# Gate rows of a mixture step: one float32 product of a token against two accumulating float32r products

## The chip, the cores and the metric

One Trainium2 chip, one of its cores. The metric is the device time of one execution in microseconds. It was run three times before the change: 4808.69, 4848.3 and 4856.97 us, median 4848.3.

## The reference

A two-layer backbone runs over 128 context tokens and 512 latent tokens of width 1024. Each layer has a token mixer (four recurrent groups) and then PEER, a mixture of 16384 single-neuron experts, of which eight heads pick 16 each for a token. The part that matters here is PEER:

```python
def peer(h, lp):
    ...
    s1 = jnp.einsum("thd,kd->thk", q[:, :, 0], lp["peer_k1"].astype(f32))
    s2 = jnp.einsum("thd,kd->thk", q[:, :, 1], lp["peer_k2"].astype(f32))
    v1, i1 = lax.top_k(s1, PEER_TOPK)
    v2, i2 = lax.top_k(s2, PEER_TOPK)
    ...
    sc, pos = lax.top_k(cand, PEER_TOPK)
    eidx = jnp.take_along_axis(cidx, pos, axis=-1)
    gate = jax.nn.softmax(sc, axis=-1)
    ...
        act = jax.nn.gelu(jnp.einsum("td,thkd->thk", xb, ub).astype(f32), approximate=False)
        return jnp.einsum("thk,thkd->td", (gb * act).astype(vb.dtype), vb)
```

An expert's number is e1 * 128 + e2, with e1 and e2 from two tables of 128 keys.

## The kernel before

**How PEER is worked.** The 128 context tokens gather their experts' rows one by one (an indirect DMA by GpSimd, a dot product by VectorE). For the 512 latent tokens the kernel computes every expert's score instead: 128 blocks of 128 experts. `score` (L1621) loads a block's weights `u`, splits them into two float32r parts, `uh` (ScalarE, L1627) and `ul` (GpSimd, a subtraction, L1628), and runs 24 float32r products of 512 columns into one PSUM bank `S` (L1632 to L1634): eight k-blocks, high by high, high by low and low by high. ScalarE's gelu takes `S` to `ring` (L1636), which goes to DRAM. `dense` (L1733) later multiplies the scores by a table of gates and by the second weights.

**The gates.** `gates_dense` (L1589) makes that table for 128 tokens at a time: for each token a 128x128 matrix over (e2, e1), zero but for the token's 128 picks, into which each pick's gate is added. It is a product over the 128 picks: `A` is one where e2 of the pick equals the column, `B` is the gate where e1 equals the column. It goes in 32 steps of four tokens. In a step VectorE writes `A` (L1605) and `C` (L1607), each by one comparison of the index row `iota` with the four tokens' picks; ScalarE turns `C` into `B` in four instructions with the gate as the scale (L1610); TensorE runs one float32 product of 128 columns a token into the bank `G` (L1613); ScalarE copies the bank to `stg` (L1614), tokens innermost there: it reads PSUM in order, and writes with a stride of 128 elements. `A` and `B` have three buffers, `C` two, `G` four.

**Ticks.** The score blocks are spread over this work. `tick` (L1682) runs one block of scores, and then issues up to two gathers of rows (`fetch`, L1658, GpSimd, paced by the block's `ul`) and uses the rows that came (`use`, L1666: VectorE's dot products into `junk`, L1670, on at most two rows less than were issued). `gates_dense` calls a tick every second step, with two gathers; `route` (L1558), which picks the experts with top-16 instructions on VectorE, calls 20, 14, 9, 9 and 9 for its five tiles of tokens. What is left of the 128 blocks of a layer runs behind the last tile.

**What sets the order.** The code is written in this order, and a scheduler then places the instructions of each engine's queue with a time line of its own; the engines run their queues in order. So gate products stand between score products on TensorE, `B` between `uh`, the gelu and the copies on ScalarE, and `A`, `C`, the dot products and the next tiles' routing on VectorE. In this text a *dense tick* is one with two gate steps (eight tokens), a *thin tick* one with some three tokens, beside the routing of a tile or where that was.

**The split.** `split` (L308) copies a tensor to its float32r part (on whichever engine the scheduler takes) and subtracts that from the whole on VectorE.

Of the kernel before, what the change touches and what calls it, by code (L numbers as in the profile page):

```python
# [9 lines left out]
F32 = mybir.dt.float32  # L10
F32R = mybir.dt.float32r
# [3 lines left out]
AF = mybir.ActivationFunctionType  # L15
ALU = mybir.AluOpType
# [12 lines left out]
P = 128  # L29
# [22 lines left out]
def _const_blocks():  # L52
# [27 lines left out]
    c["sel"] = sel  # L80
    groups = {"A": ["ident", "bones", "dtm", "fm", "nfm", "sgn"], "G": ["mL0", "mL1"], "H": ["gs", "sel"]}
    groups["R"] = ["mA0", "mA1", "rs"]
# [173 lines left out]
class Kern:  # L256
# [776 lines left out]
    def rwkv_tail(self, Y, cx):  # L1033
        nc = self.nc
        for j in range(2):
            a, b = (cx.tile([P, 12 * 128], F32, name=f"A{d}")[:, :2 * T] for d in range(2))
            sg = b.rearrange("p (z t) -> p z t", z=2)
# [11 lines left out]
    def rw_prep(self, l, d, r, k, kk, th, la, rb, omk, PC, dp, ip, tp):  # L1049
# [7 lines left out]
        for j in range(2):  # L1057
# [32 lines left out]
            for i in od:  # L1090
                A = ip.tile([P, 2, 2, 3 * 64], F32, name="A")
                for a_ in range(2):
# [3 lines left out]
                    for b in range(2):  # L1096
                        nc.tensor.matmul(pv[:, b], bk[hr, i, 2 * b:2 * b + 2].rearrange("p s t -> p (s t)"),
                                         ar[hr, j, 2 * i + b].rearrange("p s t -> p (s t)"), start=True, stop=True)
                    nc.vector.tensor_tensor(A[:, :, a_, :P], pv, self.cst(f"mA{d}")[:, None, :].to_broadcast([P, 2, P]),
                                            op=ALU.mult)  # L1100
                for b in range(2):
                    rr = slice(b * 64, b * 64 + 64)
                    nc.sync.dma_start(ad[b, i, 2 * j:2 * j + 2].rearrange("h s t -> s h t"), A[rr, b, :, :64])
                ps = self.small()
                for b in range(2):
                    nc.tensor.transpose(ps[:, b * P:(b + 1) * P],
                                        bk[:, i, 2 * b:2 * b + 2].rearrange("p s t -> p (s t)"), self.ident)
                nc.scalar.copy(A[:, :, :, P:], ps[:, :2 * P].rearrange("p (b a n) -> p b a n", b=2, a=2))
                nc.sync.dma_start(self.sA[d][:, i, :, j], A.rearrange("p b a n -> p b (a n)"))
# [479 lines left out]
    def gates_dense(self, e1, e2, gt, t0, gd, tp):  # L1589
        nc = self.nc  # L1590
        sl = tp.tile([P, 3, P], F32, name="sl")
        ps = self.small()
        for j, a in enumerate((e1, e2, gt)):
            nc.tensor.transpose(ps[:, j * P:(j + 1) * P], a, self.ident)
        nc.scalar.copy(sl, ps[:, :3 * P].rearrange("p (j n) -> p j n", j=3))
        N = 4
        io = self.iota[:, None, :].to_broadcast([P, N, P])
        stg = self.stp.tile([P, P, P], F32, name="stg")
        for t in range(0, P, N):

            def bc(j):
                return sl[:, j, t:t + N][:, :, None].to_broadcast([P, N, P])

            A = tp.tile([P, N, P], F32, name="A", bufs=3)
            nc.vector.tensor_tensor(A, io, bc(1), op=ALU.is_equal)  # L1605
            C = tp.tile([P, N, P], BF16, name="C", bufs=2)
            nc.vector.tensor_tensor(C, io, bc(0), op=ALU.is_equal)  # L1607
            B = tp.tile([P, N, P], F32, name="B", bufs=3)
            for y in range(N):
                nc.scalar.activation(B[:, y], C[:, y], AF.Copy, scale=sl[:, 2, t + y:t + y + 1])  # L1610
            ps = self.psg.tile([P, N, P], F32, name="G")
            for z in range(N):
                nc.tensor.matmul(ps[:, z], A[:, z], B[:, z], start=True, stop=True)  # L1613
            nc.scalar.copy(stg[:, :, t:t + N].rearrange("p i t -> p t i"), ps)  # L1614
            if t // N % G_TICK == 0:
                self.tick(G_FETCH, 0)
        self.stg = stg
        if t0 < NS - P:
            self.gw += [(gd[i // 8][:, :, t0:t0 + P], stg[:, i:i + 8]) for i in range(P - 8, -1, -8)]
# [310 lines left out]
```

## Time and profile before

| | us |
|---|---|
| three runs | 4808.69, 4848.3, 4856.97 |
| the profiled execution | 4822.85 |
| its span, first to last instruction | 4821.1 |
| layer 1's stretch with the gates | 930 to 1640 |
| layer 2's stretch with the gates | 3300 to 4020 |

The profile has one execution's instructions on each engine, with start, length, form, what they read and wrote, and what ended the idle time before them. PE is TensorE's products, PEld its loads of weights, DVE is VectorE, ACT ScalarE, POOL GpSimd, SP SyncE. A name ending in q is the sequencer's own instruction. A group's idle time is that of the engine just before its instructions. The ends of products are modelled, so their starts are the better measure. A float32 product appears as two records, a float32r product as one.

### The profile page before, as it was taken

Reading aid. Unit: us, or ns where it says so; the run is one execution under the profiler, and the core shown is the slowest. Engines: PE = TensorE matmul, PEld = TensorE weight load, DVE = VectorE, ACT = ScalarE, POOL = GpSimd, SP = SyncE. Lnnn points to the kernel's source line nnn. Section 1 sums busy time; section 2 is a strip of 40 time slices with the busy share of each in tenths; the row PEclk is TensorE's granted clock in tenths of the full one; section 3 lists DMA queues with packets and bytes.
Section 4 is the critical chain, followed back from the end, with each engine's and each line's share of the span. In section 5 each row is a group of like instructions: output and inputs, shape, how many; then the busy total and the mean of one; then the engine's idle time right before and its main releaser. Section 6 shows DMA issues by size and latency. Waiting matters only on the chain. (4 is left out here: it accounts for less than half of the span.)

```text
span 4821.1 us, 64797 instructions
## 1 busy us (share of the span) xinstructions
PE 4481.7 (93%) x23050; PEld 3702.0 (77%) x23050; DVE 3525.9 (73%) x6251; ACT 1912.1 (40%) x3357; POOL 2384.7 (49%) x1287
## 2 busy tenths in 40 slices
PE   7998979999999998998989899999999999999987
PEld 5786768788888876776767776887878887877775
DVE  7785478978854699996777766699795665555677
ACT  3433233446665522222233233434656664222222
POOL 2221133465666566776643212434755665665664
PEclk8996579999999999999999985999999999999998
DMA  5666141368788788888834673323878886787785
GB/s 194 189 183 205 57 143 64 123 206 268 257 274 275 254 278 297 296 282 262 296 129 120 188 222 96 119 83 117 266 252 261 267 279 229 243 257 259 257 290 175
DMA packets 504279, 1025.97 MB, mean 213 GB/s; under 512 B 80017, under 2 KB 247185, under 8 KB 502801
## 3 DMA queue, kind: packets, MB, share of 16 engines
q1 hardware_dynamic: 280112, 592.70, 38.3%
q0 software_dynamic: 75328, 275.02, 17.4%
q10 hardware_dynamic: 148514, 154.10, 9.4%
q8 instruction: 181, 2.97, 0.3%
q14 instruction: 144, 1.18, 0.1%
HBM read 841.41 MB, written 180.24 MB: 212 GB/s over the span
## 5 line engine op out<-in xcount | busy, mean ns | idle before, releaser
L1628 POOL TENSOR_TENSOR ul<-u,uh 128x1024 fp32r<-128x1024 f32 x256 | 658.6, 2573 | 661.2 <-ACT uh L1627 556.5
L1753 PE MATMUL O<-q,vh 128*128 128x512 f32 x2048 | 819.9, 401 | 102.9 <-DVE q L1775 102.4
L1754 PE MATMUL O<-qh,vl 128*128 128x512 f32 x2048 | 807.6, 395 | 23.5 <-POOL vl L1762 23.5
L1634 PE MATMUL S<-hh,ul 128*128 128x512 f32 x2048 | 813.5, 397 | 12.1 <-POOL ul L1628 12.0
L1632 PE MATMUL S<-hh,uh 128*128 128x512 f32 x2048 | 813.0, 397 | 9.3 <-ACT ring L1636 9.3
L1752 PE MATMUL O<-qh,vh 128*128 128x512 f32 x2048 | 804.3, 394 | 7.7 <-ACT qh L1774 5.3
L1762 POOL TENSOR_TENSOR vl<-v,vh 128x1024 fp32r<-128x1024 f32 x256 | 669.9, 2618 | 280.1 <-ACT vh L1761 272.2
L1633 PE MATMUL S<-hl,uh 128*128 128x512 f32 x2048 | 804.2, 393 | 0.0
L1753 PEld LDWEIGHTS O<-q,vh 128*128 128x128 f32 x2048 | 390.3, 191 | 228.5 <-DVE q L1775 148.8
L1772 DVE TENSOR_TENSOR h<-h,gt 128x384 f32<-128x384 f32 x250 | 272.1, 1089 | 372.5 <-issue 267.8
L310 POOL TENSOR_TENSOR wl<-w,wh 128x1024 fp32r<-128x1024 f32 (+1 forms) x106 | 239.1, 2261 | 551.5 <-ACT wh L309 459.2
L1774 ACT CAST qh<-h 128x512 fp32r<-128x512 f32 x250 | 154.7, 620 | 883.7 <-DVE h L1773 583.3
L1627 ACT CAST uh<-u 128x1024 fp32r<-128x1024 f32 x256 | 268.0, 1047 | 579.9 <-PE S L1633 292.6
L1670 DVE SCALAR_TENSOR_TENSOR junk<-row,hpr 128x1024 bf16<-128x1024 f32 x256 | 361.9, 1414 | 184.7 <-DMA row<-in_u_dram,ix 175.3
L1754 PEld LDWEIGHTS O<-qh,vl 128*128 128x128 f32 x2048 | 390.6, 191 | 108.4 <-POOL vl L1762 30.0
L1662 POOL DMA_INDIRECT row<-in_v_dram,ix x256 | 320.2, 1251 | 288.7 <-DVE hpr L1678 251.7
L1752 PEld LDWEIGHTS O<-qh,vh 128*128 128x128 f32 x2048 | 390.1, 191 | 92.6 <-ACT qh L1774 6.5
L1634 PEld LDWEIGHTS S<-hh,ul 128*128 128x128 f32 x2048 | 387.6, 189 | 94.1 <-POOL ul L1628 14.9
L1632 PEld LDWEIGHTS S<-hh,uh 128*128 128x128 f32 x2048 | 387.9, 189 | 85.1 <-ACT ring L1636 10.9
L1633 PEld LDWEIGHTS S<-hl,uh 128*128 128x128 f32 x2048 | 387.4, 189 | 77.3
L1678 DVE SCALAR_TENSOR_TENSOR hpr<-row,act,hpr 128x1024 f32<-128x1024 f32 x254 | 395.5, 1557 | 1.1
L296 PE MATMUL mm<-hh,wh 128*128 128x320 f32 x1184 | 383.4, 325 | 12.7 <-ACT hh L443 9.0
(449 smaller groups left out, 8639.1 us busy)
## 6 DMA issues: line engine op xcount, KB each, us to landing
u<-in_ub_dram SPq DMA_DIRECT2D x256, 512.0 KB
v<-in_v_dram SPq DMA_DIRECT2D x256, 512.0 KB
sd<-ring ACTq DMA_DIRECT2D x250, 256.0 KB
h<-sd SPq DMA_DIRECT2D x250, 256.0 KB
gd<-stg ACTq DMA_DIRECT2D x96, 512.0 KB
gt<-gd SPq DMA_DIRECT2D x256, 192.0 KB
modw<-in_modw_dram SPq DMA_DIRECT2D x88, 512.0 KB
w<-in_win_dram SPq DMA_DIRECT2D x58, 512.0 KB
```

The costliest lines, as they stand in the source:

```text
L296: nc.tensor.matmul(t[:m, :HT], a, b[:, sl], start=k == 0, stop=k == n - 1)
L1628: pp = nc.gpsimd.tensor_sub(ul, u, uh.bitcast(F32))
L1632: nc.tensor.matmul(ps, uh[:, k], xh, start=k == 0, stop=False)
L1633: nc.tensor.matmul(ps, uh[:, k], xl, start=False, stop=False)
L1634: nc.tensor.matmul(ps, ul[:, k], xh, start=False, stop=k == KC - 1)
L1662: nc.gpsimd.indirect_dma_start(out=r, out_offset=None, in_=self.I[tab], in_offset=bass.IndirectOffsetOnAxis(ap=ix[:, s:s + 1], axis=0))
L1670: nc.vector.scalar_tensor_tensor(junk, r, 1.0, hp, op0=ALU.mult, op1=ALU.mult, accum_out=act[:, s:s + 1])
L1678: nc.vector.scalar_tensor_tensor(out, r, act[:, s:s + 1], out, op0=ALU.mult, op1=ALU.add)
L1752: nc.tensor.matmul(acc[c], vh[:, sl], qh, start=z == 0, stop=False)
L1753: nc.tensor.matmul(acc[c], vh[:, sl], q, start=False, stop=False)
L1754: return nc.tensor.matmul(acc[c], vl[:, sl], qh, start=False, stop=z == NB - 1)
L1762: pace = nc.gpsimd.tensor_sub(vl, v, vh.bitcast(F32))
```

## The change

`A`, `B` and the gate become float32r. The gate row of a tile is split once into a high and a low part, `gh`. `B` gets two halves a token: the first is written by ScalarE as before, with the high part as the scale; the second by VectorE, in one instruction a token, from the index row: it compares `iota` with the pick and multiplies by the low part. TensorE then runs two float32r products of 128 columns a token on the same `A`, the second adding to the first. The copy to `stg` reads PSUM with tokens innermost (a stride of 128 elements) and writes four tokens side by side.

```diff
+        gh = tp.tile([P, 2, P], F32R, name="gh")
+        self.split(gh[:, 0], gh[:, 1], sl[:, 2])
+        gf = gh.bitcast(F32)
         stg = self.stp.tile([P, P, P], F32, name="stg")
         for t in range(0, P, N):
...
-            A = tp.tile([P, N, P], F32, name="A", bufs=3)
+            A = tp.tile([P, N, P], F32R, name="A", bufs=3)
             nc.vector.tensor_tensor(A, io, bc(1), op=ALU.is_equal)
             C = tp.tile([P, N, P], BF16, name="C", bufs=2)
             nc.vector.tensor_tensor(C, io, bc(0), op=ALU.is_equal)
-            B = tp.tile([P, N, P], F32, name="B", bufs=3)
+            B = tp.tile([P, N, 2, P], F32R, name="B", bufs=3)
             for y in range(N):
-                nc.scalar.activation(B[:, y], C[:, y], AF.Copy, scale=sl[:, 2, t + y:t + y + 1])
+                z = t + y
+                nc.scalar.activation(B[:, y, 0], C[:, y], AF.Copy, scale=gf[:, 0, z:z + 1])
+                nc.vector.tensor_scalar(B[:, y, 1], self.iota, sl[:, 0, z:z + 1], gf[:, 1, z:z + 1],
+                                        op0=ALU.is_equal, op1=ALU.mult)
             ps = self.psg.tile([P, N, P], F32, name="G")
             for z in range(N):
-                nc.tensor.matmul(ps[:, z], A[:, z], B[:, z], start=True, stop=True)
-            nc.scalar.copy(stg[:, :, t:t + N].rearrange("p i t -> p t i"), ps)
+                nc.tensor.matmul(ps[:, z], A[:, z], B[:, z, 0], start=True, stop=False)
+                nc.tensor.matmul(ps[:, z], A[:, z], B[:, z, 1], start=False, stop=True)
+            nc.scalar.copy(stg[:, :, t:t + N], ps.rearrange("p t i -> p i t"))
```

VectorE's queue in the dense ticks of a tile of the first layer, before (`junk` is the dot product of a gathered row):

```order
L1670 SCALAR_TENSOR_TENSOR junk,act<-row,hpr 128x1024
L1605 TENSOR_TENSOR A<-iota,sl 128x512 x2
L1670 SCALAR_TENSOR_TENSOR junk,act<-row,hpr 128x1024
L1607 TENSOR_TENSOR C<-iota,sl 128x512 x2
L1670 SCALAR_TENSOR_TENSOR junk,act<-row,hpr 128x1024
L1605 TENSOR_TENSOR A<-iota,sl 128x512 x2
L1670 SCALAR_TENSOR_TENSOR junk,act<-row,hpr 128x1024
```

The same place of VectorE's queue in the changed kernel, in whose line numbers A is L1608, C L1610, the second half of B L1615 and the dot product L1677:

```order
L1677 SCALAR_TENSOR_TENSOR junk,act<-row,hpr 128x1024
L1608 TENSOR_TENSOR A<-iota,sl 128x512
L1615 TENSOR_SCALAR B<-iota,sl,gh 128x128 x4
L1608 TENSOR_TENSOR A<-iota,sl 128x512
L1615 TENSOR_SCALAR B<-iota,sl,gh 128x128 x4
L1677 SCALAR_TENSOR_TENSOR junk,act<-row,hpr 128x1024
L1610 TENSOR_TENSOR C<-iota,sl 128x512 x2
```

Four new instructions stand behind each A; between them the dot products, A and C keep their places.

TensorE's queue at a thin tick of the first layer's last tile, before (S is the score, G the gates):

```order
L1632 MATMUL S<-hh,uh 128x512
L1633 MATMUL S<-hl,uh 128x512
L1613 MATMUL G<-B,A 128x128 x3
L1634 MATMUL S<-hh,ul 128x512
L1632 MATMUL S<-hh,uh 128x512
```

And in the changed kernel, where the scores are L1639 to L1641 and the two products of a token L1619 and L1620:

```order
L1640 MATMUL S<-hl,uh 128x512
L1619 MATMUL G<-B,A 128x128
L1620 MATMUL G<-B,A 128x128
L1619 MATMUL G<-B,A 128x128
L1620 MATMUL G<-B,A 128x128
L1619 MATMUL G<-B,A 128x128
L1641 MATMUL S<-hh,ul 128x512
```

Three products of three tokens became five of two and a half; they stay between the same score products, and a dense tick holds 16 where it held eight.

## Rows read from the trace of the kernel before

**Rows 1.** The page's head: span, then busy us, share and instructions of each engine.

```profile
span 4821.1 us, 64797 instructions
...
PE 4481.7 (93%) x23050; PEld 3702.0 (77%) x23050; DVE 3525.9 (73%) x6251; ACT 1912.1 (40%) x3357; POOL 2384.7 (49%) x1287
```

**Rows 2.** Windows of the two stretches: length, PE, PEld, DVE, ACT, POOL busy, clock, DMA, GB/s.

```profile
930.00:1640.00 710.00, 704.63 (x3591) 599.01 (x3592) 512.18 (x763) 437.05 (x865) 440.87 (x235) 1.00 0.77 250
3300.00:4020.00 720.00, 711.04 (x3630) 604.84 (x3629) 508.88 (x749) 439.97 (x870) 438.79 (x236) 1.00 0.77 250
```

**Rows 3.** Timeline of TensorE's products over a dense tick: start us, length us.

```profile
1423.21 1.95 PE L1613 MATMUL G<-B,A 128*128 128x128 f32 x16
...
1425.23 0.39 PE L1633 MATMUL S<-hl,uh 128*128 128x512 f32 x1
1425.46 0.39 PE L1634 MATMUL S<-hh,ul 128*128 128x512 f32 x1
...
1430.46 1.95 PE L1613 MATMUL G<-B,A 128*128 128x128 f32 x16
```

**Rows 4.** Groups by line, 930 to 1640 us: count, busy us, mean ns, idle before.

```profile
L1613 PE MATMUL G<-B,A 128*128 128x128 f32 x1016 | 130.6, 275 | 0.0
L1613 PEld LDWEIGHTS G<-B,A 128*128 128x128 f32 x1016 | 129.9, 191 | 8.7
L1607 DVE TENSOR_TENSOR C<-iota,sl 128x512 bf16<-128x512 f32 x128 | 129.9, 1035 | 38.5 <-ACT B L1610 38.5
```

**Rows 5.** Timeline of VectorE over the same tick.

```profile
1425.79 2.02 DVE L1670 SCALAR_TENSOR_TENSOR junk<-row,hpr 128x1024 bf16<-128x1024 f32 x1 [1.62 <-DMA row<-in_u_dram,ix]
...
1427.74 1.28 DVE L1605 TENSOR_TENSOR A<-iota,sl 128x512 f32<-128x512 f32 x2
1428.95 1.25 DVE L1670 SCALAR_TENSOR_TENSOR junk<-row,hpr 128x1024 bf16<-128x1024 f32 x1
...
1430.13 1.28 DVE L1607 TENSOR_TENSOR C<-iota,sl 128x512 bf16<-128x512 f32 x2
```

**Rows 6.** Timeline of GpSimd over the same tick.

```profile
1424.35 2.39 POOL L1628 TENSOR_TENSOR ul<-u,uh 128x1024 fp32r<-128x1024 f32 x1 [1.71 <-ACT uh L1627]
...
1431.59 2.41 POOL L1628 TENSOR_TENSOR ul<-u,uh 128x1024 fp32r<-128x1024 f32 x1 [1.71 <-ACT uh L1627]
```

**Rows 7.** Timeline of TensorE: float32r products of 320 columns, four between left out.

```profile
99.95 0.31 PE L296 MATMUL mm<-hl,wh 128*128 128x320 f32 x1
...
100.83 0.31 PE L296 MATMUL mm<-hl,wh 128*128 128x320 f32 x1
```

**Rows 8.** Timeline of TensorE's loads of weights: products of 65 columns.

```profile
2926.18 0.74 PEld L867 LDWEIGHTS sm<-vx,w 128*128 128x128 f32 x6 [1.48 <-DVE w L855]
```

**Rows 9.** Timeline of TensorE: a pair of records after an idle time.

```profile
462.51 0.43 PE L869 MATMUL sm<-mst,qs 64*128 64x65 f32 x2
```

**Rows 10.** Single lines of VectorE: count, ns min/median/max, first and last start, form.

```profile
L587 DVE TENSOR_SCALAR raw<-sp,cstA x2: 596/596/597, 102.3 to 2521.8; 64x640 f32<-64x640 f32 x2
L485 DVE TENSOR_SCALAR gr<-ge x2: 484/486/487, 78.8 to 2506.7; 64x640 f32<-64x640 f32 x2
L1574 DVE TENSOR_SCALAR ab<-pos x20: 210/220/2432, 866.9 to 3562.4; 128x128 uint32<-128x128 uint32 x20
L1523 DVE MAX8 s<-mr x80: 365/428/431, 846.1 to 3556.0; 128x8 f32<-128x256 f32 x80
```

**Rows 11.** Single lines of ScalarE: a read of a PSUM bank in order; the copy to stg.

```profile
L1636 ACT ACTIVATE ring<-S x256: 582/592/625, 818.3 to 4026.5; 128x512 f32<-128x512 f32 x128
L1614 ACT COPY stg<-G x256: 1058/1083/1172, 944.4 to 4010.5; 128x512 f32<-128x512 f32 x128
```

**Rows 12.** Windows: a run of thin ticks, columns as in rows 2.

```profile
1300.00:1360.00 60.00, 59.27 (x292) 49.70 (x292) 20.42 (x26) 33.61 (x60) 23.40 (x10) 1.00 0.87 269
```

**Rows 13.** Waits, 930 to 1640 us: us in total, times, longest us.

```profile
DVE A L1605 <- PE G L1613: 33.0, 11, 8.5
```

## The prediction

> **What bounds the kernel now.** I read the head of the page first: TensorE is busy 93% of the span, every other engine less [rows 1]. The change touches only the stretch in which the gates of the 512 latent tokens are built, once in each layer; I cut that out of the table of windows. There TensorE is busy 704.6 of 710 us and 711.0 of 720 us, at a granted clock of 1.00 (its 2.4 GHz level), while VectorE is busy 512 and 509 us [rows 2]. So a microsecond that TensorE loses in these 1430 us is a microsecond of the kernel, and one that it saves counts only if nothing else is late next.
>
> Then I read the stretch as a period, in the timeline. In the dense part one tick goes with two gate steps: 24 score products and eight tokens. The gate products are one row of 16 records from 1423.21 us, and the next such row begins at 1430.46: a period of 7.25 us [rows 3]. The records of one row stand (1.95 - 0.275) / 15 = 0.112 us apart; 1024 tokens give 2048 records [rows 3, 4]: each float32 product runs as two records, 0.223 us a token. A score product comes 0.227 us after the last [rows 3].
>
> In the same period VectorE works: two A (1.21 us from the first start to what follows), a dot product (1.18), two C (1.2) and a second dot product (1.2), 4.8 us in all [rows 5]. GpSimd's subtraction for `ul` takes 2.39 us [rows 6]. These two exclude each other: the dot product that starts at 1425.79 takes 2.02 us instead of 1.25, and ends 1.07 us after the subtraction's end at 1426.74 [rows 5, 6]; C averages 1035 ns in this stretch though the pair takes 1.28 [rows 4, 5]. Before that dot product VectorE idled 1.62 us for its gathered row [rows 5], and that idle time lies beside the subtraction. So 4.8 + 2.4 = 7.2 us of the 7.25 are already taken on VectorE. TensorE is the bound, but VectorE with GpSimd is a second one at almost the same height. This is the main point of the forecast.
>
> **The change part by part.** *The products.* 1024 float32 products go, 2048 float32r products of 128 columns come: as many records as now. The trace has no float32r product under 320 columns. Bounds: going by columns alone, 320 take 0.147 us start to start (six in 0.88 us) and 512 take 0.227, 0.42 ns a column, so 128 would take 0.067 us [rows 3, 7]. But each record also loads 128 columns of weights. The loads of the 65-column products on 128x128 weights stand (0.74 - 0.19) / 5 = 0.110 us apart, as far as the gates' records of 128 columns [rows 3, 8]: there the load, not the columns, sets the pace. Two such products in a row after an idle time even stand 0.43 - 0.27 = 0.16 us apart [rows 4, 9]. I take 0.111 us, the row nearest in kind (back-to-back, 128x128 weights, few columns): 2048 x (0.112 - 0.111) is nothing. Ends: -0.045 x 2048 = -92 us and +0.048 x 2048 = +98 us.
>
> The Trainium skill, TensorE: Matmul & The Clock Gate, section "LDWEIGHTS (loading the stationary operand)", prices a load by its columns alone, 107 ns for 128; the 0.110 us of rows 8 agree. The same page's section "Back-to-back issue gap" gives about 81 ns a product for a sustained stream at 128 columns; by that TensorE would save some 63 us (an estimate from that page). No row here shows 128-column loads closer than 0.11 us, so the trace sides with the first rule.
>
> *The second half of B on VectorE.* 1024 one-input TENSOR_SCALAR of 128 columns with two pointer scalars are added, eight a dense tick. A 640-column one with two pointers takes 596 ns; without pointers 640 columns take 486 and 128 columns 220 [rows 10]. The slope is 266 / 512 = 0.52 ns a column, so 596 - 266 = 330 ns, less the 0.08 us by which neighbours on VectorE overlap (a pair of A takes 1.28, not 2 x 0.68): 0.25 us each, 2.0 us a tick. Bounds: 0.14 us (the 220 ns without pointers) and 0.33 us. Does it run beside GpSimd's subtraction? A TENSOR_SCALAR of the same size stretches from 220 to 2432 ns in this stretch, MAX8 never goes past 431 [rows 10]. So it waits like A and C do.
>
> The Trainium skill, SBUF — State Buffer, section "Who interferes with whom", says that a VectorE instruction with one SBUF input is free of GpSimd outside the two-port modes, and that tensor_scalar can enter those. If these ran in the free mode, up to 2.0 us a tick would lie under the subtraction and the change would cost nothing; if not, it costs the sum below. The 2432 ns of rows 10 speak for the second.
>
> *The order.* In the changed kernel VectorE's queue reads dot product, A, four TENSOR_SCALAR, A, four more, dot product, two C; nothing else changes place. Behind a late TENSOR_SCALAR wait A, C and the dot products; behind a late C wait ScalarE's B and, queued behind those, the cast `uh`, then GpSimd's `ul`, then the score products. A late VectorE therefore stops TensorE as a whole, not just the gates.
>
> *ScalarE.* B stays four instructions a step. The copy to `stg` now writes four tokens side by side and reads PSUM with the stride: between 592 ns (an unstrided read of 128x512 from PSUM) and 1083 + 491 ns if the strided read costs what the strided write did [rows 11]. Two a tick: -1.0 to +1.0 us on an engine busy 437 of 710 us [rows 2]. I cost it at nothing: VectorE's period of 9.2 us (below) covers it, and without that cover it would cost up to 1.0 us less what ScalarE idles now. *The split of the gate row:* two short instructions a tile, eight tiles, at most 5 us, beside score products: nothing. A as float32r: same elements, nothing.
>
> **The sum.** Dense tick: 4.8 + 2.0 + 2.4 = 9.2 us of VectorE with GpSimd against 7.2 now: +2.0 us. The new TensorE order holds 92 ticks' worth of eight tokens (736 of the 1024) over both layers: +184 us. Taken off: in the thin ticks (three tokens) VectorE idles (20.4 busy of 60 us) and runs ahead until A has no free buffer (33 us of waits for the gate products) [rows 12, 13]. It enters six of the eight dense parts some two steps ahead, 7 us: -42 us. Added: in two tiles of each layer the thin ticks lie beside routing, with VectorE full; 44 ticks x 3 x 0.25 = 33 us, of which I take half: +16. Sum: +158 us. The profiled execution took 4822.9 us, which gives 4981; it lies 25 us under the median of the three runs (4848.3), on which scale it would be 5006. I say 4995.
>
> **The rivals.**
> *Hidden (no change).* The TENSOR_SCALAR slip under GpSimd's subtraction or into VectorE's idle 1.62 us, and TensorE still sets 7.25. For it: MAX8, also with one input, is never stretched, and no TENSOR_SCALAR of this very form is in the trace. Against: the stretched ones of rows 10, and that the idle time lies beside the subtraction. Time: 4823 to 4848.
> *Faster.* The float32r records run at 0.067 us, as the columns say. TensorE's dense tick falls to 24 x 0.227 + 16 x 0.067 = 5.45 + 1.07 = 6.5 us. For it: the column slope, which nothing in the trace breaks between 320 and 512. Against: rows 8. It decides only once VectorE with GpSimd falls below 7.2, that is if the additions are free and the dot products move under the subtraction too; then the whole -92 us counts: 4731 to 4756. (The Trainium skill's 81 ns, TensorE: Matmul & The Clock Gate, section "Back-to-back issue gap", belongs to this rival.) If only the additions are free, 7.2 stands, and the gain is that of the 288 tokens outside the dense ticks, 288 x 2 x 0.045 = 26 us, within what can be told from no change.
> *Dearer products.* The second product of a token waits for the first, 0.16 us a record [rows 9]. Against it: the score products accumulate too, and follow each other without a gap [rows 3]. The dense tick of TensorE is then 5.45 + 16 x 0.16 = 8.0, still under 9.2, so only the thin ticks pay: 288 x 2 x 0.048 = +28 us on top of the forecast, 5023; where a record costs a whole float32 product, 0.223, the dense tick is 9.0 and the thin tokens cost 288 x 0.223 = +64: 5059.
>
> **How the numbers follow.** Forecast 0.65; hidden 0.16; dearer products 0.11; faster 0.08. A measurement of this kernel tells about 1% from no change (4800 to 4897). Faster by more: the last case, 0.08. Within it: the hidden case and 0.02 of the forecast, where an addition costs least, 0.18. Slower by more: 0.63 and 0.11, 0.74. The likeliest case alone spans 4905 to 5120: 0.14 us an addition makes 92 x 1.1 - 42 + 9 = +68, and 0.33 us without any lead makes 92 x 2.6 + 44 = +283, each between the two scales. The whole range is 4815 (hidden, with a part of the 26 us of cheaper products) to 5145 (the +283 on the median's scale and a little for dearer products); the faster case lies outside it.
>
> **What would show it.** Right: the gate products' records still 0.11 us apart; the new TENSOR_SCALAR near 330 ns at the median with some over 2 us; dense ticks of about 9 us with VectorE full and TensorE idle before gate products, waiting for B; the two stretches each some 80 us longer and all else as it was. Wrong: records at 0.06 us; a dense tick that stays at 7.25 us; TENSOR_SCALAR that never stretch; time lost outside the two stretches; or ScalarE's copy as what the gate products wait for.

## The result and the profile after

The changed kernel takes 4981.35 us (median of four executions, 4944.74 to 4987.46) against 4832.22 (four executions of the kernel before beside them): a ratio of 1.029, 95% interval 1.025 to 1.034. It is slower by 2.9%. The forecast was 4995 us.

The head of the changed kernel's page, as [rows 1]:

```profile
span 4981.5 us, 65843 instructions
...
PE 4555.3 (91%) x23050; PEld 3754.3 (75%) x23050; DVE 3927.4 (79%) x7283; ACT 1811.7 (36%) x3363; POOL 2374.6 (48%) x1287
```

The span grows by 160.4 us. TensorE has as many products as before, 23050; VectorE has 1032 instructions and 402 us more; ScalarE is busy 100 us less. The two stretches with the gates, as [rows 2] (length, PE, PEld, DVE, ACT, POOL busy, clock, DMA, GB/s):

```profile
930.00:1720.00 790.00, 743.09 (x3621) 626.85 (x3620) 720.30 (x1261) 390.57 (x871) 432.77 (x236) 0.96 0.70 226
3390.00:4180.00 790.00, 739.98 (x3595) 623.64 (x3594) 713.71 (x1250) 389.68 (x870) 429.87 (x235) 0.95 0.70 227
```

The stretches became 790 us long, from 710 and 720. TensorE now idles some 50 us in each, at a lower granted clock, and VectorE, idle 198 of 710 us before, idles 70 of 790. The gates' products span 698.6 us before and 774.7 now in the first layer, 697.7 and 775.1 in the second (first to last start): 153.5 of the 160.4 us are in there.

TensorE's timeline at the gate products of a dense tick (start us, length us), as [rows 3]:

```profile
1494.66 0.40 PE L1641 MATMUL S<-hh,ul 128*128 128x512 f32 x1
1494.90 0.22 PE L1619 MATMUL G<-B,A 128*128 128x128 f32 x1
1494.96 0.27 PE L1620 MATMUL G<-B,A 128*128 128x128 f32 x1
1495.07 0.28 PE L1619 MATMUL G<-B,A 128*128 128x128 f32 x1
1495.18 0.28 PE L1620 MATMUL G<-B,A 128*128 128x128 f32 x1
...
1496.52 0.28 PE L1620 MATMUL G<-B,A 128*128 128x128 f32 x1
1496.63 0.44 PE L1639 MATMUL S<-hh,uh 128*128 128x512 f32 x1
```

From the second record to the last it is 1.56 us for 14 steps, 0.111 us each: what the float32 records took in [rows 3]. VectorE's new instructions (count, ns min/median/max, first and last start):

```profile
L1615 DVE TENSOR_SCALAR B<-iota,sl,gh x1024: 328/335/3000, 936.2 to 4167.9; 128x128 fp32r<-128x128 f32 x171
```

VectorE over one dense tick, as [rows 5], from one A to the A that stands at the same place of the next tick:

```profile
1494.65 0.68 DVE L1608 TENSOR_TENSOR A<-iota,sl 128x512 fp32r<-128x512 f32 x1
1495.26 1.10 DVE L1615 TENSOR_SCALAR B<-iota,sl,gh 128x128 fp32r<-128x128 f32 x4
1496.28 0.68 DVE L1608 TENSOR_TENSOR A<-iota,sl 128x512 fp32r<-128x512 f32 x1
1496.88 3.18 DVE L1615 TENSOR_SCALAR B<-iota,sl,gh 128x128 fp32r<-128x128 f32 x4
1499.99 1.21 DVE L1677 SCALAR_TENSOR_TENSOR junk<-row,hpr 128x1024 bf16<-128x1024 f32 x1
...
1501.13 1.28 DVE L1610 TENSOR_TENSOR C<-iota,sl 128x512 bf16<-128x512 f32 x2
1502.34 1.21 DVE L1677 SCALAR_TENSOR_TENSOR junk<-row,hpr 128x1024 bf16<-128x1024 f32 x1
...
1503.48 0.68 DVE L1608 TENSOR_TENSOR A<-iota,sl 128x512 fp32r<-128x512 f32 x1
```

The tick is 1503.48 - 1494.65 = 8.83 us, without an idle moment on VectorE. Over all 88 dense ticks of the trace VectorE idles less than 0.1 us a tick on the mean; in e1 below, which has the same order without the additions, it idles 1.46 of 7.25 us. Four additions take 1.02 us start to start where nothing is beside them (1495.26 to 1496.28), and 3.11 us at 1496.88. GpSimd says why, as [rows 6]:

```profile
1488.15 2.49 POOL L1635 TENSOR_TENSOR ul<-u,uh 128x1024 fp32r<-128x1024 f32 x1 [3.17 <-ACT uh L1634]
...
1496.96 2.50 POOL L1635 TENSOR_TENSOR ul<-u,uh 128x1024 fp32r<-128x1024 f32 x1 [3.17 <-ACT uh L1634]
```

The subtraction begins 0.08 us behind the first of these four. That first one still takes its usual 335 ns; the second, begun at 1497.14, takes 2412 ns, and ends 0.09 us behind the subtraction. And ScalarE's timeline shows what a late C holds up (in brackets: the idle time before, and what ended it):

```profile
1493.02 0.40 ACT L1614 ACTIVATE B<-C,gh 128x128 fp32r<-128x128 bf16 x1 [3.99 <-DVE C L1610]
...
1494.67 1.27 ACT L1614 ACTIVATE B<-C,gh 128x128 fp32r<-128x128 bf16 x4
1495.85 1.03 ACT L1634 CAST uh<-u 128x1024 fp32r<-128x1024 f32 x1
```

C, then B, then the cast `uh`, then `ul`: the ring is closed, since `ul` stops VectorE, which makes the next C late. In the list of waits (us in total, times, longest us) of the first stretch:

```profile
POOL ul L1635 <- ACT uh L1634: 271.1, 89, 8.8
ACT B L1614 <- DVE C L1610: 170.6, 44, 9.3
```

### The profile page after: what moved, and what is told of

Its sections match the earlier page's. It is cut to its first block, busy times and chain, and to the rows that moved or that the text cites. A ratio compares the mean times of both kernels' runs of the same rounds, so it can differ in the third digit from the quotient of the medians.

```text
span 4981.5 us, 65843 instructions
## 1 busy us (share of the span) xinstructions
PE 4555.3 (91%) x23050; PEld 3754.3 (75%) x23050; DVE 3927.4 (79%) x7283; ACT 1811.7 (36%) x3363; POOL 2374.6 (48%) x1287
## 5 line engine op out<-in xcount | busy, mean ns | idle before, releaser
L1641 PE MATMUL S<-hh,ul 128*128 128x512 f32 x2048 | 829.7, 405 | 20.7 <-POOL ul L1635 20.6
L1639 PE MATMUL S<-hh,uh 128*128 128x512 f32 x2048 | 831.0, 406 | 15.6 <-ACT ring L1643 15.6
L1640 PE MATMUL S<-hl,uh 128*128 128x512 f32 x2048 | 822.5, 402 | 0.0
L1615 DVE TENSOR_SCALAR B<-iota,sl,gh 128x128 fp32r<-128x128 f32 x1024 | 507.9, 559 | 0.0
L1641 PEld LDWEIGHTS S<-hh,ul 128*128 128x128 f32 x2048 | 398.9, 195 | 106.6 <-POOL ul L1635 23.3
L1639 PEld LDWEIGHTS S<-hh,uh 128*128 128x128 f32 x2048 | 400.9, 196 | 96.3 <-ACT ring L1643 18.8
L1640 PEld LDWEIGHTS S<-hl,uh 128*128 128x128 f32 x2048 | 399.9, 195 | 82.6
L1614 ACT ACTIVATE B<-C,gh 128x128 fp32r<-128x128 bf16 x1024 | 327.1, 393 | 360.1 <-DVE C L1610 353.3
```

Of the source, the lines that this page charges most:

```text
L1614: nc.scalar.activation(B[:, y, 0], C[:, y], AF.Copy, scale=gf[:, 0, z:z + 1])
L1615: nc.vector.tensor_scalar(B[:, y, 1], self.iota, sl[:, 0, z:z + 1], gf[:, 1, z:z + 1], op0=ALU.is_equal, op1=ALU.mult)
L1639: nc.tensor.matmul(ps, uh[:, k], xh, start=k == 0, stop=False)
L1640: nc.tensor.matmul(ps, uh[:, k], xl, start=False, stop=False)
L1641: nc.tensor.matmul(ps, ul[:, k], xh, start=False, stop=k == KC - 1)
```

## The experiments

Times are medians; the ratio is to executions of the kernel before on the same chip (medians of 4820 to 4836 us). The span of the gates is that of their products in the first layer, first to last start. The dense tick is counted in the trace, from the first of 24 score products to the next such first, where eight tokens' gate products start in between; its median stands here.

| kernel | us | ratio, 95% interval | span of the gates, us | dense tick, us |
|---|---|---|---|---|
| before | 4832 | 1 | 698.6 | 7.25 |
| changed | 4981 | 1.029, 1.025 to 1.034 | 774.7 | 8.83 |
| e1_no_low | 4842 | 1.006, 1.004 to 1.007 | 704.6 | 7.25 |
| e2_added | 5009 | 1.040, 1.036 to 1.043 | 787.9 | (other order) |
| e3_copy | 4828 | 1.000, 0.996 to 1.003 | 708.2 | 7.25 |
| e4_one | 4792 | 0.994, 0.992 to 0.997 | 684.1 | 6.46 |
| e5_psum | 4968 | 1.028, 1.025 to 1.032 | 773.8 | 8.44 |
| e6_act | 4844 | 1.000, 0.997 to 1.003 | 710.7 | 7.25 |
| e7_no_ul | 4862 | 1.007, 1.004 to 1.010 | 716.3 | 7.25 |
| e8_before_no_ul | 4861 | 1.005, 1.002 to 1.009 | 705.4 | 7.25 |
| e9_one_c16 | 4790 | 0.990, 0.987 to 0.993 | 676.2 | 6.72 |
| e10_half | 4885 | 1.009, 1.006 to 1.013 | 727.5 | 7.91 |
| e11_double | 5301 | 1.096, 1.093 to 1.099 | 940.5 | 11.25 |
| e12_one_no_ul | 4734 | 0.978, 0.973 to 0.982 | 643.8 | 6.35 |

**e1_no_low: without the additions.**

```diff
-                nc.vector.tensor_scalar(B[:, y, 1], self.iota, sl[:, 0, z:z + 1], gf[:, 1, z:z + 1],
-                                        op0=ALU.is_equal, op1=ALU.mult)
...
-                nc.tensor.matmul(ps[:, z], A[:, z], B[:, z, 1], start=False, stop=True)
+                nc.tensor.matmul(ps[:, z], A[:, z], B[:, z, 0], start=False, stop=True)
```

> The changed kernel without VectorE's 1024 new instructions: both products of a token read the first half of B (the low part of the gate is left out, the high part counts twice). TensorE, ScalarE and the copy work as in the changed kernel. Theory (the new instructions, together with GpSimd's subtraction, fill VectorE): the dense tick returns from 8.8 to about 7.25 us, each stretch from 790 to about 710 us, and the time to 4800 to 4870 us, as before the change. Rival, dearer products: the time stays above 4900 us, since all 2048 products are still there. Rival, the copy: if the new order of the copy costs something, the time stays up too.

Measured: 4842 us, the dense tick at 7.25 us in 88 ticks, as many as the changed kernel has of them. The wait of B for C is down from 170.6 us:

```profile
ACT B L1614 <- DVE C L1610: 19.8, 10, 7.6
```

All 2048 products are still there, and the copy is the new one: neither the products nor the copy make the loss, the additions do. Of the 0.6% that is left, 11 us are in the gates' spans of both layers (1407 against 1396 us); where the rest is stays open, for the profiled executions have a span of 4823.7 us here and 4821.1 before.

**e2_added: the additions alone, in the kernel before.**

```diff
+            for y in range(N):
+                nc.vector.tensor_scalar(A[:, y], self.iota, sl[:, 0, t + y:t + y + 1], sl[:, 2, t + y:t + y + 1],
+                                        op0=ALU.is_equal, op1=ALU.mult)
             nc.vector.tensor_tensor(A, io, bc(1), op=ALU.is_equal)
```

> The kernel before with 1024 instructions of the new form added to VectorE and nothing else: they write into A's buffer just before A itself overwrites it, so no other engine waits for one more semaphore, and the float32 products and the old copy stay. Theory: about what the change costs, 4930 to 5010 us, with stretches of 770 to 800 us and the instructions at a median near 335 ns, some over 2 us. Rival (the loss comes from the products, or from their wait for a second writer of B): within 1% of before, 4785 to 4880 us.

Measured: 5009 us, at the upper end of what the theory gave.

```profile
L1606 DVE TENSOR_SCALAR A<-iota,sl x1024: 320/336/3151, 946.4 to 4184.7; 128x128 f32<-128x128 f32 x171
```

The additions alone, with the float32 products and the old copy, cost as much as the whole change. They cost a little more, and the scheduler placed the products differently: 31 of its ticks hold twelve tokens and only 24 eight. What the other order adds was not separated. So this run shows the cause, and the price only roughly.

**e3_copy: the copy alone.**

```diff
-            nc.scalar.copy(stg[:, :, t:t + N].rearrange("p i t -> p t i"), ps)
+            nc.scalar.copy(stg[:, :, t:t + N], ps.rearrange("p t i -> p i t"))
```

> The kernel before with the new order of the copy to stg alone. Theory: the copy falls from 1083 to about 572 ns, ScalarE was not what the tick waits for, and the time stays within 1% of before (4785 to 4880 us), the dense tick at 7.25 us. Rival: ScalarE's 2 x 0.51 us a dense tick stand on the path from C over B to the cast uh, and the time falls by up to 92 x 1.0 = 92 us, to about 4740 us.

Measured: no difference (0.996 to 1.003), though the copy takes little more than half of its 1083 ns:

```profile
L1614 ACT COPY stg<-G x256: 558/577/612, 930.5 to 4010.1; 128x512 f32<-128x512 f32 x128
```

So 256 x 0.5 = 128 us of ScalarE are worth nothing while TensorE sets the tick.

**e6_act: the low half by ScalarE.** Nothing of the change is missing but who writes the second half of B.

```diff
-                nc.vector.tensor_scalar(B[:, y, 1], self.iota, sl[:, 0, z:z + 1], gf[:, 1, z:z + 1],
-                                        op0=ALU.is_equal, op1=ALU.mult)
+                nc.scalar.activation(B[:, y, 1], C[:, y], AF.Copy, scale=gf[:, 1, z:z + 1])
```

> The changed kernel with the second half of B written by ScalarE too, from C with the low part as the scale; VectorE has no added instruction, nothing is left out. ScalarE gets 8 more instructions of 0.32 us a dense tick, and has saved 2 x 0.51 us in the copies: 4.5 - 1.0 + 2.5 = 6.0 of 7.25 us. Theory (the loss is VectorE's): the dense tick returns to about 7.3 us, the time to 4810 to 4880 us. Rival (the loss is that uh and the gelu are late, and ScalarE's order makes them late again, being behind eight more instructions): 4900 to 5000 us.

Measured: 4844 us, a ratio of 1.000. Two products a token, float32r, the split and 1024 more instructions on ScalarE together cost nothing that can be measured. The loss is that of the engine chosen.

**e7_no_ul and e8_before_no_ul: both kernels without GpSimd's subtraction.** The same edit in each:

```diff
-        ul = self.up.tile([P, KC, P], F32R, name="ul", bufs=2)
...
-        pp = nc.gpsimd.tensor_sub(ul, u, uh.bitcast(F32))
+        pp = pa
...
-            nc.tensor.matmul(ps, ul[:, k], xh, start=False, stop=k == KC - 1)
+            nc.tensor.matmul(ps, uh[:, k], xh, start=False, stop=k == KC - 1)
```

> The changed kernel without GpSimd's subtraction: the low part of the second weights is left out, the third score product reads the high part again, and the gathers are paced by the cast. All 1024 new instructions stay on VectorE. Theory (VectorE's time and the subtraction add up, 4.8 + 2.0 + 2.4): without the 2.4 us VectorE needs 6.8 us a dense tick, under TensorE's 7.25, so the two stretches go back by 60 to 75 us each and the time to 4810 to 4870 us, and none of the new instructions takes over 1 us. Rival (VectorE's plain time alone makes the tick late, through the order of its queue): 4920 us or more.

> The kernel before without GpSimd's subtraction, as the partner of the changed kernel without it (low part of the second weights left out). TensorE's products set its dense tick already, so both theories expect little: 4780 to 4850 us. What counts is the distance to its partner: under 40 us if the subtraction and VectorE's additions only hurt together, over 80 us if the additions hurt by themselves.

Measured: 4862 and 4861 us. The 149 us between the two medians shrink to 1, with all 1024 additions in place and none of them over 550 ns:

```profile
L1615 DVE TENSOR_SCALAR B<-iota,sl,gh x1024: 328/341/550, 939.5 to 4038.8; 128x128 fp32r<-128x128 f32 x171
```

The dense tick is at TensorE's 7.25 us in both. The spans of the gates, both layers together, are 1431.1 and 1410.1 us: of the 153.5 us between the two kernels 21 are left there, and the executions of each scatter by 30 to 40 us. This is the clearest of the runs: with the subtraction gone most of what the additions cost goes too, and what is left can't be told from nothing by the times. The edit also takes `ul` out of the chain from C to the score products, so it alone does not tell VectorE's lost time from that delay; that VectorE has no idle moment in the changed kernel's dense tick does. e8 came out 11 us above the range that was given for it, and why was not found; that it is no faster than the kernel before says that there the subtraction was hidden.

**e5_psum: the index row read from PSUM.**

```diff
-                    self.psg = en3(self.pool("psg", 4, space=PSUM))
+                    self.psg = en3(self.pool("psg", 3, space=PSUM))
+                    iop = en3(self.pool("iop", 1, space=PSUM))
+                    self.iop = iop.tile([P, P], F32, name="iop")
+                    nc.scalar.copy(self.iop, self.iota)
...
-                nc.vector.tensor_scalar(B[:, y, 1], self.iota, sl[:, 0, z:z + 1], gf[:, 1, z:z + 1],
+                nc.vector.tensor_scalar(B[:, y, 1], self.iop, sl[:, 0, z:z + 1], gf[:, 1, z:z + 1],
```

> The changed kernel, but VectorE's new instructions read the index row from a copy in PSUM (the gate products have three PSUM buffers for that, not four). Theory as on record (the added instructions wait for GpSimd's subtraction because both use the same way into SBUF): reading PSUM they run beside it, their longest fall from 3000 to under 700 ns, their 2.0 us a dense tick lie under the 2.39 us of the subtraction, the dense tick falls from 8.8 to some 7.4 us and the time to 4830 to 4890 us. Rival (what costs is VectorE's own time, or the exclusion doesn't care where the operand stands): 4950 to 5020 us, as the changed kernel.

Measured: 4968 us, not the theory's 4830 to 4890 but inside the rival's range. The instructions did what the theory says of them, and the time did not follow:

```profile
L1615 DVE TENSOR_SCALAR B<-iop,sl,gh x1024: 390/398/409, 927.6 to 4153.3; 128x128 fp32r<-128x128 f32 x171
```

Not one in 1024 is stretched. The exclusion does care where the operand stands. But the timeline (VectorE, then GpSimd) shows what that bought:

```profile
1473.03 1.35 DVE L1615 TENSOR_SCALAR B<-iop,sl,gh 128x128 fp32r<-128x128 f32 x4
1474.31 2.14 DVE L1677 SCALAR_TENSOR_TENSOR junk<-row,hpr 128x1024 bf16<-128x1024 f32 x1
```

```profile
1472.87 2.50 POOL L1635 TENSOR_TENSOR ul<-u,uh 128x1024 fp32r<-128x1024 f32 x1 [0.82 <-ACT uh L1634]
```

The four additions run beside the subtraction for 1.28 us; then comes a dot product, which reads two tensors of SBUF, meets the remaining 1.06 us and takes 2.14 us for its 1.21. And from PSUM an addition takes 1.28 / 4 = 0.32 us instead of 0.255. So the median tick of eight tokens falls by 0.4 us to 8.44 (83 ticks), not to 7.4. Even that hardly shows in the time: the ticks with about two tokens (three to five of the gates' products), 40 in either kernel, take 6.58 us on the mean instead of 6.14, 18 us in all, and the order is another one. Whether three PSUM buffers in place of four are to blame for that was not tried.

**e10_half and e11_double: half and twice the additions.** In e10 a condition `if y % 2 == 0:` stands ahead of VectorE's instruction, and the second product reads `B[:, z, 1 - z % 2]`; in e11 four more stand ahead of A, as in e2.

> The changed kernel with half of VectorE's added instructions: for two of four tokens the second half of B is VectorE's, for the other two the first half of B is used twice (the low part of their gates is left out), so TensorE, ScalarE and the copy do what they do in the changed kernel. Theory (each addition counts by itself, 0.25 us, from a VectorE that was full before): half of the loss, 4890 to 4925 us. Rival (a wait that tips over once VectorE is late): nearly all of the loss, over 4945 us, or hardly any, under 4870 us.

> The changed kernel with 1024 more instructions of the same form on VectorE (written into A's buffer just before A overwrites it; nothing is left out). Theory: the same price again, and a little more, since the thin ticks have no room left: 0.25 us x 736 to 1024 is 184 to 256 us on top of the changed kernel's 4981, 5150 to 5240 us. Rival (one wait a tick, whatever the number): 4980 to 5060 us.

Measured: 4885 and 5301 us; both miss the theory's ranges, by 5 us below and 61 us above. The order of e10 is that of the changed kernel (88 dense ticks each), and there the steady tick goes 7.25, 7.91 and 8.83 us with 0, 4 and 8 additions. From 7.91 to 8.83 an addition costs 0.92 / 4 = 0.23 us. Drawn back from there, VectorE with GpSimd needs 7.91 - 0.92 = 7.0 us with none (8.83 - 2.04 = 6.8 if each takes the 0.255 us of the timeline), 0.25 to 0.45 less than TensorE's 7.25, so the first one or two of a tick are hidden and each further one counts. That is a second bound that has passed the first, not a wait that tips over. In e11 1024 more cost 320 us, 0.31 us each, more than they take: A's buffer is taken earlier (62 us of the additions' waits are for gate products), and here the thin ticks are longer too. How much belongs to which was not separated.

**e4_one, e9_one_c16 and e12_one_no_ul: one product a token.** e4 is the changed kernel without the additions and the second product:

```diff
-                nc.tensor.matmul(ps[:, z], A[:, z], B[:, z, 0], start=True, stop=False)
-                nc.tensor.matmul(ps[:, z], A[:, z], B[:, z, 1], start=False, stop=True)
+                nc.tensor.matmul(ps[:, z], A[:, z], B[:, z, 0], start=True, stop=True)
```

> The changed kernel with one float32r product a token: VectorE's new instructions and the second product go, so the low part of the gate is left out. TensorE has 1024 records fewer: at 0.111 us that is 114 us, and a dense tick of 24 x 0.227 + 8 x 0.111 = 6.3 us on TensorE. Theory: VectorE with GpSimd's subtraction (4.8 + 2.4 = 7.2 us) holds the dense tick at 6.9 to 7.25 us, so only part of it shows: 4750 to 4815 us, with TensorE idle in the dense ticks. Rival (TensorE alone sets the tick, VectorE and GpSimd don't exclude each other): the dense tick goes to 6.3 us and the time to 4690 to 4735 us.

Measured: 4792 us, 0.994 (0.992 to 0.997). Half of the gates' records are gone, and a quarter of their 114 us is gained. The time is in the theory's range, but the dense tick is not: its median is 6.46 us, not 6.9 to 7.25. The order is another one, with eight tokens in only 48 ticks; 25 of them go at TensorE's pace, 6.35 us on the mean, and 23 take 6.93. Other ticks, beside the routing of a layer's first two tiles, take 11 to 15 us. e9 adds bf16 copies of the index row and the picks, and compares those for C:

> The kernel with one float32r product a token and no added VectorE instructions (the low part of the gate is left out), and with C compared from bf16 copies of the index row and the picks, 128 and below, which bf16 holds exactly. Theory (VectorE with GpSimd holds that kernel's dense tick at some 7.0 us, TensorE alone would need 6.3): if a C falls from 0.6 to about 0.35 us, the tick loses up to 0.5 us and the time goes to 4730 to 4775 us; if C takes as long from bf16, it stays at 4775 to 4810 us. Rival (something else holds that kernel): C falls and the time stays above 4775 us.

Measured: 4790 us, 0.990 (0.987 to 0.993); the interval overlaps that of e4. C takes the same from bf16, so nothing was taken from VectorE:

```profile
L1613 DVE TENSOR_TENSOR C<-i x256: 665/681/3529, 947.6 to 3978.4; 128x512 bf16<-128x512 bf16 x128
```

e12 is e4 with the edit of e7.

> The kernel with one float32r product a token and no added VectorE instructions, now also without GpSimd's subtraction (left out: the low part of the gate, and the low part of the second weights, whose product reads the high part again). Its partners are the two kernels without the subtraction and with all products, 4861 to 4862 us. Theory (a gate record costs TensorE 0.11 us, and one product a token gained only some 30 us because VectorE and GpSimd together held the tick): TensorE is now the only bound, and the 1024 records less show in full, 1024 x 0.11 = 114 us: 4735 to 4775 us. Rival (records cost less than 0.11 us, or TensorE waits for something else): over 4800 us.

Measured: 4734 us, 127 us under e7 and e8, which ran on another chip (the kernel before took 4834 us on either). That is 1 us under the range. With GpSimd's subtraction out of the way TensorE's 1024 records show in full, and the dense tick is 6.35 us, what the sum for TensorE gave (6.3). So 0.11 us a record holds, and what held e4 back goes with the subtraction; how much of it was VectorE's time in the dense ticks and how much the late ticks beside the routing was not separated. e4 and e9 are the versions that beat both kernels, at the price of the gate's low part; e12 leaves out too much to be one.

## Why the prediction was right, and where its steps were off

*The products: right.* The records are 0.111 us apart, as the loads of weights said [rows 8], not 0.067 as the columns would have it ([rows 7] have five products between the two shown, not four, so six steps of 0.147 us are right); e6 shows that the pair of products costs nothing, and e12 that a record is worth 127 / 1024 = 0.12 us. The faster rival and the dearer products fall with that. The Trainium skill's figure of 81 ns for a sustained stream at 128 columns (TensorE: Matmul & The Clock Gate, section "Back-to-back issue gap") appears in none of these runs: behind its first step, no longer row of the gates' products is closer than 0.111 us a product.

*The additions: right in size and kind.* 335 ns against 330 forecast, 0.255 us each in the tick against 0.25. They are stretched to as much as 3000 ns beside the subtraction, and with it gone at most 21 of the 153.5 us in the gates' spans are left (e7 against e8). The hidden rival had MAX8 for it, which is never stretched; the additions are not like it. The Trainium skill (SBUF — State Buffer, section "Who interferes with whom") says that a tensor_scalar can contend with GpSimd, if its operands meet conditions; the trace agrees for an input in SBUF, and e5's 409 ns at the most show no contention with the input in PSUM.

*The dense tick: the subtraction's term was too big.* "4.8 + 2.0 + 2.4 = 9.2 us" measured 4.7 + 2.04 + 2.09 = 8.83: of the subtraction's 2.5 us VectorE loses only 2.09, since the addition under way when it begins is finished beside it (335 ns), and the one that is held ends 0.09 us behind it, not a whole 0.33. So VectorE's need without additions was 6.8 to 7.0 us (e10), not the "7.2 us of the 7.25" of the forecast: 0.25 to 0.45 us a tick were free. The ticks of eight tokens are 88, not 92, so the term is 1.58 x 88 = 139 us, not 184.

*The lead and the routing: the step that failed.* "-42" was for VectorE running ahead in the thin ticks and entering the dense part two steps early. The lead is there: 23 of the 88 dense ticks take under 7.5 us, most of them the first one to three of a tile. But most of it is given back at once. The dense ticks of the first layer's third tile of latent tokens take 7.3, 7.2, 7.5, 12.2, 8.9, 7.2 and 8.3 us, 58.6 in seven, where seven steady ones take 61.8: a lead of some 3 us, not 7. When the lead is used up, one tick pays for several. Over the six dense parts other than those of the second tiles the time lies 19 us under 8.83 us a tick.

The tiles beside routing lose on the other side. The first four dense ticks of the second tile take 17.5, 11.6, 12.5 and 9.0 us, and the second tiles of both layers together lie 26 us above the steady 8.83. The kernel before has a late tick at the same place, 11.6 us in the first layer and 15.9 in the second, 13 us above its steady 7.25; so +13 is new. The ticks with fewer than eight tokens take 34 us more than their products need (24 x 0.227 us and 0.1115 a record), against 13 before: +21, of which 17 are in the first tile of each layer. That is +34 where the forecast had +16. Not all of it is the additions' doing: e1, with the new order and without them, is 11 us above the kernel before in these spans.

So 139 - 19 + 34 = 154 us in the gates' spans stand against 184 - 42 + 16 = 158 forecast, and the profiled executions differ by 160. The mechanism was right, but that the number came so near is luck: two errors go against each other, 45 us too much in the tick and 41 too little for the lead and the routing. The 7 us outside the spans are as much as the profiled executions of the other kernels differ by.

*ScalarE at nothing: right.* The copy is not dearer but cheaper, a little under the 592 ns that the forecast had as its lower bound:

```profile
L1621 ACT COPY stg<-G x256: 556/572/607, 938.4 to 4173.6; 128x512 f32<-128x512 f32 x128
```

Its 1.0 us a dense tick buys nothing where TensorE sets the tick (e3); with VectorE as the bound it was not tried.

## What to carry to other kernels

An engine that is idle 28% of a stretch can still be full: look at one period, add to its busy time what another engine takes from it, and compare that sum with the bound. Here VectorE had 0.25 to 0.45 of 7.25 us to give, while ScalarE, with some 40% idle, took the same work for nothing. And when a product is rewritten in more parts, count the loads of weights first: two float32r products of 128 columns cost TensorE what one float32 product did, so nothing was there to win that could have paid for the operands.

## What was not expected of the hardware

*A strided read of PSUM costs ScalarE nothing extra, a strided write to SBUF does.* The copy took 1083 ns writing with a stride of 128 elements [rows 11], and takes 572 ns reading PSUM with that stride and writing four elements side by side; a read in order (the gelu [rows 11]) takes 592.

*TensorE's clock falls after its waits.* In the kernel before the granted clock was 1.00 in both stretches. In the changed one it is 0.96 and 0.95, and the timeline shows where:

```profile
1485.19 0.28 PE L1620 MATMUL G<-B,A 128*128 128x128 f32 x1
1486.67 0.30 PE L1619 MATMUL G<-B,A 128*128 128x128 f32 x1 [1.20 <-ACT B L1614]
...
1489.21 0.63 PE L1641 MATMUL S<-hh,ul 128*128 128x512 f32 x1
1489.63 0.63 PE L1639 MATMUL S<-hh,uh 128*128 128x512 f32 x1
...
1492.16 0.39 PE L1639 MATMUL S<-hh,uh 128*128 128x512 f32 x1
1492.39 0.40 PE L1640 MATMUL S<-hl,uh 128*128 128x512 f32 x1
```

Two us behind an idle time of 1.20 us the score products stand 0.42 us apart for some 3 us, and then again 0.23: the 1.2 and the 2.4 GHz level. So TensorE, which was made to wait, was slower afterwards as well. What this adds to the loss was not measured by itself; it falls in ticks that VectorE sets, so it may be little.

*C is as slow from bf16 as from float32.* 681 ns against 682, where both inputs repeat elements and go through the same comparison (e9 and e4).
